# First layer of a two-layer trunk on one core: startup transfers, two projections' weights in the gated buffer, rotation's scaling on ACT, retention's scores two tiles ahead

## The chip, the core and the metric

The kernel runs on one core of a Trainium2 chip. The core has a matrix engine (PE, with its weight loads listed as PEld), a vector engine (DVE), an activation engine (ACT), a general engine (POOL) and a queue engine (SP). Each works through its own instructions in order and waits on semaphores for the others; transfers run on 16 DMA engines. The metric is the device time of one execution in microseconds (us); the median of several runs counts.

## The reference, cut to what matters

One inference step over 576 tokens (a prompt of 512 and 64 tokens of a running stream), width 1024, fp32. Layer 0 runs four heads of mLSTM and four heads of retention behind one input projection; layer 1 is latent attention; each is followed by a SwiGLU network.

```
z = x @ w_in_a     # mLSTM q, k, v, o; gates i, f; retention q, k, v, g
q, k = rope(q_ret, pos), rope(k_ret, pos)          # rotation
S_t = gamma_h * S_{t-1} + k_t^T v_t ; o_t = q_t S_t # retention, per head
h_ret = head_norm(o) * g_ret ; y = concat(h_mlstm, h_ret * silu(g)) @ w_out_a
```

Retention is computed in chunks: scores q k^T under a mask with the decay, times v, plus the state's part. The powers of gamma that belong to single rows are put into q and k right after the rotation: this is the "scaling" below.

## The kernel before, in words

Every fp32 product is made as three products of reduced-precision parts. A number is split into a high part (ACT casts it) and a low part (DVE subtracts, or POOL in other stages). For weights `split` does this (`L364` on ACT, `L362` on DVE), for x `split_x` (`L600`, `L601`, tiles `Xh`, `Xl`). Weights arrive in blocks of 512 KB through three raw buffers (`dma_w`, `L342`); a block is split in pieces ("fills") of 512 columns into slots of a ring (tiles `r0` to `r8`). Where a fill goes, and whether a slot is free, `claim` decides from the last fill that is still needed (`hold`); `pins` binds a fill to given slots, `L0_SLOTS` lists those of layer 0. `prefetch` emits splits ahead of use, up to `lead` fills.

The tokens stand in five tiles: tile 0 is the stream's 64, tiles 1 to 4 have 128 each. x comes in two halves, of 320 and 256 tokens; the first holds tiles 0 to 2, the second (x') tiles 3 and 4. What each engine does in which order follows from the order in which the program emits it. The stretch around the change runs so:

1. `rqrk`, retention's q and k: tiles 1 and 2 are multiplied k block by k block while weights and x arrive. Then the gates' product over the first half (`gate_mm(0)`), tile 0, tile 3, `gate_mm(1)`, tile 4. `tm_units` emits each tile as two units of four k blocks; `ev_qk` takes a finished tile out of its PSUM bank (`mm`): DVE rotates it (`L697` to `L700`) and scales q (`L702`) and k (`L704`), and a unit later PE transposes both (`L533`) and ACT copies the result to `qkT` (`L714`).
2. The gates: ACT copies their rows out of PSUM (`L660`) and PE transposes them; a task (`gates`, `L829` to `L911`) goes on with them, next to the following projections.
3. `rv` and `mv`, the values of retention and mLSTM, five tiles each. During `mv` five tasks of `retention` are interleaved, one for each tile: `s1` (scores in two PSUM banks, DVE multiplies by the mask, `L928`), `s2` (scores times values plus the state, the state's update, `L950` to `L959`, and the head norm, `L964` to `L970`) and `s3` (transposes and a copy).
4. Then mLSTM's `mk`, `mq`, `mo` and the gate `rg`, head by head.

PSUM has three banks called `mm`, four called `x` and one called `o`. The buffer `H` will hold the gated values; it is not in use this early, but for the columns from 8192 on. `T0`, `T1` and `Z` are working buffers with several uses one after another.

Of the kernel before, what the change touches and what calls it, by code (L numbers as in the profile page):

```python
# [8 lines left out]
F32 = mybir.dt.float32  # L9
# [8 lines left out]
KT = 8  # L18
# [19 lines left out]
NT = 5  # L38
# [7 lines left out]
RING = range(16)  # L46
LOW = range(8)
OUT_SLOTS = (range(8, 10), range(14, 16), range(10, 12), range(12, 14))
L0_SLOTS = (0, 1, 2, 3, 4, 5, 6, 7, 14, 15)
MLA_SLOTS = range(6)  # L50
LEAD = 5
LEAD_SLOTS = (8, 9, 14, 15, 0, 1, 2, 3, 4, 5, 6, 7)
# [165 lines left out]
class Kern:  # L218
    def __init__(self, ctx, tc, t):
        self.tc, self.nc, self.t = tc, tc.nc, t  # L220
        self.sb = ctx.enter_context(tc.tile_pool(name="sb", bufs=1))
        self.pm = ctx.enter_context(tc.tile_pool(name="pm", bufs=PM, space=bass.MemoryType.PSUM))
        self.px = ctx.enter_context(tc.tile_pool(name="px", bufs=PX, space=bass.MemoryType.PSUM))
        self.po = ctx.enter_context(tc.tile_pool(name="po", bufs=1, space=bass.MemoryType.PSUM))
        ctx.enter_context(tc.manual_schedule())
        self.n = 0
        self.bg = []
        self.clk = 0.0
        self.plan = Plan()
# [195 lines left out]
    def prefetch(self, i, lead, qlead=QLEAD):  # L425
        last = len(self.plan.fills) - 1
        self.load()
        while True:
            while self.split_next in self.done:
                self.split_next += 1  # L430
            j = self.split_next
            if j > min(i + (lead if j > last or len(self.plan.fills[j]) == 3 else qlead), last):
                return
            if not self.attempt(j):
                assert j > i, (i, self.hold, self.slot_of, self.plan.fills[j][0] in self.raws, self.pins.get(j))
                return
# [117 lines left out]
    def setup(self):  # L554
        nc, t = self.nc, self.t
        self.lead = LEAD
        self.lo_engine = nc.vector
        self.tk = TK0
        self.Z = self.st("Z", [128, KT * NTOK])
        self.T0 = self.st("T0", [128, T0_N])  # L560
        self.T1 = self.st("T1", [128, T1_N])
        self.Xh = self.st("Xh", [128, KT * NTOK], F32R)
        self.Xl = self.st("Xl", [128, KT * NTOK], F32R)
        self.H = self.st("H", [128, 2 * KT * NTOK], F32R)
        self.small = self.st("small", [128, 480])
# [12 lines left out]
        nc.gpsimd.memset(self.cvec[:, 2:4], 1.0 / 512.0)  # L578
        self.wgp = self.st("wgp", [128, KT, 16], F32R)
        for j in range(4):  # L580
            for k in (2 * j, 2 * j + 1) if j == 0 else (2 * j,):
                e = k + 1 if j == 0 else k + 2
                nc.sync.dma_start(half_view(self.Z, 0, k, e), half_dram(t["x"], 0, k, e))
                if j < RAW and k % 2 == 0:
                    self.dma_w(j, 2 if j == 0 else 1)

        x = self.obank()
        for _ in range(8):
            self.mm(x[:, 0:128], self.ones, self.ones, True, True)
# [4 lines left out]
        self.nc.scalar.copy(hi, wg)  # L594
        self.nc.vector.tensor_tensor(self.wgp[:, :, 8:16], wg, hi.bitcast(F32), ALU.subtract)

    def split_x(self, half, ks):
        for k in ks:
            a, b = hcols(half, k)
            self.nc.scalar.copy(self.Xh[:, a:b], self.Z[:, a:b])  # L600
            self.nc.vector.tensor_tensor(self.Xl[:, a:b], self.Z[:, a:b], self.Xh[:, a:b].bitcast(F32), ALU.subtract)  # L601

    def xs(self, half, cut=HN[0]):
        def f(k):
# [17 lines left out]
    def layer0(self):  # L622
# [38 lines left out]

        half_sum = Z[0:64, 3972:4484]

        def tm_units(name, evac, tiles=range(NT)):
            for i in tiles:
                box = {}

                def first(i=i, box=box):
                    self.rel = i == NT - 1
                    if i == 0 and name != "rqrk":  # L670
                        self.start((name, 0))
# [11 lines left out]
        def ev_qk(i, ps):  # L683
# [14 lines left out]
            V.tensor_tensor(t2[:, :, 0:32], p3[:, :, 32:64], S[:, :, 0:32].to_broadcast([L, 8, 32]), ALU.mult)  # L698
            V.tensor_tensor(t2[:, :, 32:64], p3[:, :, 0:32], S[:, :, 32:64].to_broadcast([L, 8, 32]), ALU.mult)  # L699
            V.tensor_tensor(t1, t1, t2, ALU.add)  # L700
            gam = self.cst[0:L, 0:8].unsqueeze(2)
            V.tensor_tensor(t1[:, 0:4, :], t1[:, 0:4, :], gam[:, 0:4, :].to_broadcast([L, 4, 64]), ALU.mult)  # L702
            kt = self.ktok[0:L, i, :].rearrange("p (h d) -> p h d", h=4)
            V.tensor_tensor(kt, t1[:, 4:8, :], gam[:, 4:8, :].to_broadcast([L, 4, 64]), ALU.mult)  # L704

            def g():
                x = self.xbank()
# [27 lines left out]

        self.XS = self.H[:, 8192:9216].rearrange("p (k t) -> p k t", k=KT)
        banks = [None, self.bank(), self.bank()]
        for k in range(KT):
            self.lead = 1 - k % 2 if k < KT - 1 else LEAD
            self.split_x(0, [k])  # L740
            if k == KT - 1:
                self.split_wg()
                self.split_x(1, range(KT))
            if k % 4 == 3:
                self.pair_sample(k - 3, k + 1)
            for i in (1, 2):
                self.tm(banks[i][0:TLEN[i], :], "rqrk", [k], self.xt(i), first=k == 0, last=k == KT - 1)
                if k == KT - 1:
                    ev_qk(i, banks[i])
            if k == 3:  # L750
                for name in ("rope", "ident", "mask", "cst"):
                    nc.sync.dma_start(getattr(self, name), t[name])
                nc.sync.dma_start(T0[:, 4300:4364], t["wg"])
                nc.sync.dma_start(self.bif, t["b_if"].to_broadcast([128, 8]))
            if k in (3, 4):
                j = k - 3
                nc.sync.dma_start(half_view(Z, 1, 4 * j, 4 * j + 4), half_dram(t["x"], 1, 4 * j, 4 * j + 4))
        for dst, name in ((self.sel, "sel"), (self.reset, "reset"), (self.m0, "m0"), (self.CxS, "c0"), (self.S[0], "s0"),
                          (self.gv, "gv"), (self.lnv, "lnv")):
            nc.sync.dma_start(dst, t[name])  # L760
        nc.gpsimd.tensor_scalar(self.gv, self.gv, 0.5, None, ALU.mult)
        gate_mm(0)
        tm_units("rqrk", ev_qk, (0,))
        tm_units("rqrk", ev_qk, (3,))
        gate_mm(1)
        self.gates_done = False
        self.spawn(self.gates(grow), 1.0)
        tm_units("rqrk", ev_qk, (4,))
        tm_units("rv", ev_rv)
        rt = self.retention()  # L770
        for g in rt:
            self.spawn(g)
# [3 lines left out]

        for x in (mva[64:128, 0], mvb[64:128, 0], r7[64:128, 1290:1418], r6[:, 1029:1157]):
            nc.gpsimd.memset(x, 0.0)
        tm_units("mv", ev_mv)

        done = set()
        self.ml_done = [0] * 4
# [131 lines left out]
    def retention(self):  # L914
# [5 lines left out]

        def s1(i):
            L, s = TLEN[i], TSTART[i]
            for o, bank in enumerate((self.obank(), self.bank())):
                x3 = bank[:, 0:256].rearrange("p (a t) -> p a t", a=2)
                p0 = 64 * o
                for a in range(2):
# [4 lines left out]
        def s2(i):  # L931
# [19 lines left out]
            for a in range(2):  # L951
                for p0 in (0, 64):
# [32 lines left out]
        self.ret_at = at  # L985

        def task(i):
            while at["s1"] < i or at["s2"] < i - 1 or self.qk_done < NT:
                yield
            s1(i)  # L990
            at["s1"] += 1
            yield LAG["r1"]
            while at["s2"] < i or at["s3"] < i - 1:
                yield
            if at["t2"] + LAG["r3"] > self.clk:
                yield at["t2"] + LAG["r3"] - self.clk
            s2(i)
            at["s2"] += 1
            at["t2"] = self.clk
            yield LAG["r2"]  # L1000
# [1262 lines left out]
```

## Time and profile before

| | us |
|---|---|
| median of 3 runs | 1393.08 (1391.89 to 1393.73) |
| the profiled execution | 1393.54 |
| its span, first to last instruction | 1391.6 |
| PE busy | 1351.7 |
| DVE busy | 979.5 |
| ACT busy | 610.8 |

Busy time is the time in which an engine has an instruction at work; the span is a little shorter than the execution, which has a start and an end around it. The mean clock granted to PE is 0.992 of full speed. In the lists below a row of the timeline gives start, length, engine, line of the program, operation, output and inputs, and in brackets the idle time of that engine just before it, with the instruction that ended it. A row of waits gives the sum, the number and the longest.

### The profile page before, as it was taken

Reading aid. Unit: us, or ns where it says so; the run is one execution under the profiler, and the core shown is the slowest. Engines: PE = TensorE matmul, PEld = TensorE weight load, DVE = VectorE, ACT = ScalarE, POOL = GpSimd, SP = SyncE. Lnnn points to the kernel's source line nnn. Section 1 sums busy time; section 2 is a strip of 40 time slices with the busy share of each in tenths; the row PEclk is TensorE's granted clock in tenths of the full one; section 3 lists DMA queues with packets and bytes.
Section 4 is the critical chain, followed back from the end, with each engine's and each line's share of the span. In section 5 each row is a group of like instructions: output and inputs, shape, how many; then the busy total and the mean of one; then the engine's idle time right before and its main releaser. Section 6 shows DMA issues by size and latency. Waiting matters only on the chain.

```text
span 1391.6 us, 24628 instructions
## 1 busy us (share of the span) xinstructions
PE 1351.7 (97%) x9759; PEld 1305.6 (94%) x9759; DVE 979.5 (70%) x2277; ACT 610.8 (44%) x1295; POOL 155.0 (11%) x182
## 2 busy tenths in 40 slices
PE   8999999999999999999999999999999999999995
PEld 6778999999999999999987899999999999999995
DVE  6757677678873685588898565667888358647876
ACT  4422333445551453255354466543555235425533
POOL 1100001115000000000021533311320000000000
PEclk9999999999999999999999999999999999999997
DMA  6121122611232123223321000021213312222221
GB/s 218 61 61 55 47 75 59 194 60 61 88 108 79 62 103 109 76 92 95 117 86 59 31 31 31 32 92 44 94 61 108 106 61 92 91 91 77 93 75 68
DMA packets 38234, 112.91 MB, mean 81 GB/s; under 512 B 5024, under 2 KB 12512, under 8 KB 38120
## 3 DMA queue, kind: packets, MB, share of 16 engines
q1 hardware_dynamic: 38120, 111.35, 24.3%
q8 instruction: 76, 1.25, 0.4%
q14 instruction: 38, 0.31, 0.1%
HBM read 107.45 MB, written 3.89 MB: 80 GB/s over the span
## 4 chain that ended last, share of the span: by engine, by line
PE 83%; DVE 10%; ACT 3%; DMA 2%; issue 2%; POOL 0%; SPq 0%; POOLq 0%; ACTq 0%; DVEq 0%
PE mm L465 44%; PE x L465 36%; PE x L533 2%; DVE r L362 2%; DVE Z L1279 1%; DMA raw<-in_w 1%; DVE Z L1265 1%; PE o L465 1%; ACT Xh L1311 1%; DMA Z<-in_x 1%; ACT r L364 0%; ACT Z L1318 0%; DVE small L542 0%; DVE small L541 0%; DVE small L543 0%
## 5 line engine op out<-in xcount | busy, mean ns | idle before, releaser
L465 PE MATMUL mm<-H,r 128*128 128x320 f32 (+2 forms) x2832 | 387.6, 297 | 0.0
L465 PEld LDWEIGHTS mm<-H,r 128*128 128x128 f32 x2832 | 378.3, 189 | 0.3
L465 PE MATMUL x<-Xh,r 128*128 128x288 f32 x1216 | 244.7, 296 | 0.0
L465 PE MATMUL mm<-Xh,r 128*128 128x288 f32 (+2 forms) x1152 | 229.2, 297 | 6.4 <-DVE Z L1185 2.8
L364 ACT CAST r<-raw 128x512 fp32r<-128x512 f32 (+2 forms) x292 | 178.0, 646 | 104.6 <-PE mm L465 76.0
L362 DVE TENSOR_TENSOR r<-raw,r 128x512 fp32r<-128x512 f32 (+2 forms) x276 | 194.4, 733 | 38.0 <-ACT r L364 37.8
L465 PE MATMUL x<-r,r 128*128 128x288 f32 (+2 forms) x1534 | 211.7, 293 | 0.2 <-DVE r L1055 0.2
L465 PEld LDWEIGHTS x<-r,r 128*128 128x128 f32 x1534 | 205.9, 188 | 0.5 <-DVE r L1055 0.5
L465 PEld LDWEIGHTS x<-Xh,r 128*128 128x128 f32 x1216 | 194.6, 188 | 0.5
L465 PEld LDWEIGHTS mm<-Xh,r 128*128 128x128 f32 x1152 | 183.4, 189 | 7.7 <-ACT Z L1318 3.8
L465 PE MATMUL x<-Xl,r 128*128 128x288 f32 x608 | 179.5, 295 | 0.0
L465 PE MATMUL mm<-Xl,r 128*128 128x288 f32 (+2 forms) x576 | 167.1, 298 | 0.0
L364 ACT CAST r<-T 128x512 fp32r<-128x512 f32 (+1 forms) x114 | 86.9, 762 | 127.5 <-DVE T L397 112.0
L465 PEld LDWEIGHTS x<-Xl,r 128*128 128x128 f32 x608 | 114.1, 188 | 0.0
L362 DVE TENSOR_TENSOR r<-T,r 128x512 fp32r<-128x512 f32 (+1 forms) x114 | 96.3, 866 | 18.6 <-ACT r L364 18.6
L465 PEld LDWEIGHTS mm<-Xl,r 128*128 128x128 f32 x576 | 107.2, 189 | 0.1
L465 PE MATMUL mm<-r,Xh 128*128 128x512 f32 (+1 forms) x320 | 98.8, 391 | 4.6 <-DVE r L699 2.6
L1319 POOL TENSOR_TENSOR Xl<-Z,Xh 128x288 fp32r<-128x288 f32 (+2 forms) x36 | 30.7, 853 | 467.0 <-ACT Z L1318 466.5
L465 PEld LDWEIGHTS mm<-r,Xh 128*128 128x128 f32 x320 | 58.8, 192 | 17.9 <-issue 3.0
L1223 ACT ACTIVATE T<-Z 128x288 f32<-128x288 f32 (+2 forms) x56 | 24.8, 443 | 91.8 <-DVE Z L1185 47.4
L465 PE MATMUL mm<-r,Xl 128*128 128x512 f32 (+1 forms) x160 | 61.3, 383 | 0.0
L1580 DVE TENSOR_TENSOR T<-T,x 128x288 f32<-128x288 f32 x38 | 17.2, 453 | 59.1 <-PE x L465 59.1
(316 smaller groups left out, 1725.9 us busy)
## 6 DMA issues: line engine op xcount, KB each, us to landing
raw<-in_w SPq DMA_DIRECT2D x169, 512.0 KB, 3.5
r<-in_w SPq DMA_DIRECT2D x20, 512.0 KB, 3.4
Z<-in_x SPq DMA_DIRECT2D x1, 1280.0 KB
o_y<-Z SPq DMA_DIRECT2D x2, 640.0 KB, 3.3
Z<-in_x SPq DMA_DIRECT2D x2, 512.0 KB, 7.2
Z<-in_x SPq DMA_DIRECT2D x1, 1024.0 KB, 8.7
o_y<-Z SPq DMA_DIRECT2D x4, 256.0 KB, 2.1
Z<-in_x SPq DMA_DIRECT2D x3, 320.0 KB, 4.9
```

The costliest lines, as they stand in the source:

```text
L362: self.lo_engine.tensor_tensor(t[:, 1], src, t[:, 0].bitcast(F32), ALU.subtract)
L364: self.nc.scalar.copy(t[:, 0], src)
L465: self.nc.tensor.matmul(out, lhsT, rhs, start=start, stop=stop, skip_group_check=more)
L533: self.nc.tensor.transpose(out, in_, self.ident[0:n, 0:n])
L1223: nc.scalar.activation(q, z, AF.Square)
L1265: V.tensor_tensor(z, z, xd[:, 0:n], ALU.subtract)
L1279: V.scalar_tensor_tensor(z, z, gain(m), R[:, 0:n], ALU.mult, ALU.mult)
L1311: A.activation(self.Xh[:, a:b], z, AF.Identity, bias=bias(m))
L1319: G.tensor_tensor(self.Xl[:, a:b], z, self.Xh[:, a:b].bitcast(F32), ALU.subtract)
L1580: V.tensor_tensor(s[:, 0:n], s[:, 0:n], ps, ALU.add)
```

## The change

*Transfers.* The first three transfers of x go out on ACT's queue, the weights on SP's alone. x' is loaded into `T1` right after the first k block is emitted, ahead of the tables (`rope`, `ident`, `mask`, `cst`), the gates' weights and biases. Before, it came behind these, into `Z`.

*Slots.* The fills of `rqrk` and `mv` are pinned to `H`, so that all ten slots of the ring serve `rv` and what comes after `mv`. A new bound, `cap`, limits how far ahead splits are emitted.

*Splits of x'.* Half of them follow the rotation of tile 1, half that of tile 2; before, all eight stood ahead of both.

*Scaling.* Instead of two DVE multiplications a tile, eight ACT instructions, each over 64 columns with a factor per row.

*Retention.* The scores of tile 1 use an `x` bank, so those of tile 0 and 1 need not share `o`. `s2` is cut in two, and the scores of tile i+2 are emitted between the state's update and the norm (`s2b`).

```diff
-L0_SLOTS = (0, 1, 2, 3, 4, 5, 6, 7, 14, 15)
+L0_SLOTS = (6, 7, 14, 15, 0, 1, 2, 3, 4, 5)
...
+        self.cap = len(self.plan.fills)
+        for k in range(KT):
+            for nm in ("rqrk", "mv"):
+                self.pins[self.where[(nm, k)][0]] = (len(RING) + k,)
...
-            if j > min(i + (lead if j > last or len(self.plan.fills[j]) == 3 else qlead), last):
+            if j > min(i + (lead if j > last or len(self.plan.fills[j]) == 3 else qlead), last, max(i, self.cap)):
...
-                nc.sync.dma_start(half_view(self.Z, 0, k, e), half_dram(t["x"], 0, k, e))
+                (nc.scalar if j < 2 else nc.sync).dma_start(half_view(self.Z, 0, k, e), half_dram(t["x"], 0, k, e))
...
+                    self.cap = self.where[(name, KT - 1)][0] + ahead * (1 if len(tiles) == 1 else i + 1)
...
-            gam = self.cst[0:L, 0:8].unsqueeze(2)
-            V.tensor_tensor(t1[:, 0:4, :], t1[:, 0:4, :], gam[:, 0:4, :].to_broadcast([L, 4, 64]), ALU.mult)
-            V.tensor_tensor(kt, t1[:, 4:8, :], gam[:, 4:8, :].to_broadcast([L, 4, 64]), ALU.mult)
+            for j in range(8):
+                nc.scalar.activation(t1[:, j, :] if j < 4 else kt[:, j - 4, :], t1[:, j, :], AF.Copy, scale=self.cst[0:L, j:j + 1])
...
-                self.split_x(1, range(KT))
+        for i in (1, 2):
+            ev_qk(i, banks[i])
+            self.split_x(1, range(4 * i - 4, 4 * i), x1)
...
-        tm_units("rqrk", ev_qk, (0,))
-        tm_units("rqrk", ev_qk, (3,))
+        self.lead = 2 * KT
+        tm_units("rqrk", ev_qk, (0,), 2)
+        tm_units("rqrk", ev_qk, (3,), 5)
...
-            for o, bank in enumerate((self.obank(), self.bank())):
+            for o, bank in enumerate((self.xbank() if i == 1 else self.obank(), self.bank())):
...
-            s2(i)
+            O = s2(i)
+            if i + 2 < NT:
+                s1(i + 2)
+            s2b(i, O)
```

PE's instructions keep their number and order; some read other tiles. Three places show what moves on the two engines that feed PE. Names are those of the tiles with numbers that tell their uses apart; `x4` stands for four alike. First ACT around the copy of the second gates (`T<-x 16x256`), before:

```order
L364 CAST r_35_231<-raw_30_145 128x512
L364 CAST r_36_234<-raw_30_145 128x512
L660 COPY T_3_71<-x_265 16x320
L527 COPY Z_69<-mm_283 64x512
L714 COPY Z_69<-x_321 128x4x128
L714 COPY Z_69<-x_327 128x4x128
L660 COPY T_3_71<-x_351 16x256
L714 COPY Z_69<-x_382 128x4x64
```

The same stretch of ACT now:

```order
L371 CAST r_33_284<-raw_28_151 128x512 x2
L534 COPY Z_69<-mm_283 64x512
L713 ACTIVATE r_24_112<-r_24_112,cst_83 64x64 x4
L713 ACTIVATE Z_69<-r_24_112,cst_83 64x64 x4
L371 CAST r_36_322<-raw_29_175 128x512
L371 CAST r_37_325<-raw_29_175 128x512
L371 CAST r_39_330<-raw_30_197 128x512
L723 COPY Z_69<-x_345 128x4x128
L723 COPY Z_69<-x_351 128x4x128
L713 ACTIVATE r_24_112<-r_24_112,cst_83 128x64 x4
L713 ACTIVATE Z_69<-r_24_112,cst_83 128x64 x4
L668 COPY T_3_71<-x_381 16x256
```

Between the two gate copies stood three copies; now the scaling of tile 0 and of tile 3 and five casts of weights stand there too. Second, DVE after the rotation of tile 1, before:

```order
L601 TENSOR_TENSOR Xl_73<-Z_69,Xh_72 128x256 x8
L362 TENSOR_TENSOR r_35_231<-raw_30_145,r_35_231 128x512
L362 TENSOR_TENSOR r_36_234<-raw_30_145,r_36_234 128x512
L697 TENSOR_TENSOR r_24_112<-mm_113,rope_82 128x512
L698 TENSOR_TENSOR r_24_112<-mm_113,rope_82 128x8x32
L699 TENSOR_TENSOR r_24_112<-mm_113,rope_82 128x8x32
L700 TENSOR_TENSOR r_24_112<-r_24_112 128x512
L702 TENSOR_TENSOR r_24_112<-r_24_112,cst_83 128x256
L704 TENSOR_TENSOR Z_69<-r_24_112,cst_83 128x256
L697 TENSOR_TENSOR r_24_112<-mm_114,rope_82 128x512
```

and now:

```order
L707 TENSOR_TENSOR r_24_112<-mm_113,rope_82 128x512
L708 TENSOR_TENSOR r_24_112<-mm_113,rope_82 128x8x32
L709 TENSOR_TENSOR r_24_112<-mm_113,rope_82 128x8x32
L710 TENSOR_TENSOR r_24_112<-r_24_112 128x512
L609 TENSOR_TENSOR Xl_73<-T_3_71,Xh_72 128x256 x4
L707 TENSOR_TENSOR r_24_112<-mm_114,rope_82 128x512
```

The rotation of tile 1 (`mm_113`) has moved ahead of the splits of x', of which four follow it, and its scaling has left this engine. Third, DVE in retention, the end of tile 2's norm, before:

```order
L970 TENSOR_SCALAR r_24_112<-x_872,small_75 128x128
L970 TENSOR_SCALAR r_24_112<-x_873,small_75 128x128
L928 TENSOR_TENSOR r_24_112<-o_909,mask_81 128x2x128
L928 TENSOR_TENSOR r_24_112<-mm_910,mask_81 128x2x128
L950 TENSOR_TENSOR Z_69<-Z_69,cst_83 128x256
```

and now:

```order
L986 TENSOR_SCALAR r_24_112<-x_914,small_75 128x128
L986 TENSOR_SCALAR r_24_112<-x_915,small_75 128x128
L369 TENSOR_TENSOR r_39_330<-raw_67_688,r_39_330 128x512 x2
L962 TENSOR_TENSOR Z_69<-Z_69,cst_83 128x256
L971 SCALAR_TENSOR_TENSOR Z_69<-x_984,cst_83,Z_69 64x128 x2
```

The masks of the scores to come have left this place (they stand ahead of the norm now), and two splits of weights have come to it, as they have after tiles 1 and 3; before, these splits followed the norm of tile 4.

More of the change, by code (lines that the diff above doesn't have):

```diff
@@ L326, in slot @@
     def slot(self, s):
+        if s >= len(RING):
+            o = 2 * FILL * (s - len(RING))
+            return self.H[:, o:o + 2 * FILL].rearrange("p (e c) -> p e c", e=2)
         b = self.buffer(s)
@@ L595, in split_wg, with split_x @@
         self.nc.vector.tensor_tensor(self.wgp[:, :, 8:16], wg, hi.bitcast(F32), ALU.subtract)
-    def split_x(self, half, ks):
+    def split_x(self, half, ks, src=None):
         for k in ks:
             a, b = hcols(half, k)
-            self.nc.scalar.copy(self.Xh[:, a:b], self.Z[:, a:b])
-            self.nc.vector.tensor_tensor(self.Xl[:, a:b], self.Z[:, a:b], self.Xh[:, a:b].bitcast(F32), ALU.subtract)
+            x = self.Z[:, a:b] if src is None else src[:, k, :]
+            self.nc.scalar.copy(self.Xh[:, a:b], x)
+            self.nc.vector.tensor_tensor(self.Xl[:, a:b], x, self.Xh[:, a:b].bitcast(F32), ALU.subtract)
     def xs(self, half, cut=HN[0]):
@@ L662, in layer0, with tm_units @@
         half_sum = Z[0:64, 3972:4484]
-        def tm_units(name, evac, tiles=range(NT)):
+        def tm_units(name, evac, tiles=range(NT), ahead=LEAD):
             for i in tiles:
@@ L737, in layer0 @@
         banks = [None, self.bank(), self.bank()]
+        x1 = T1[:, 0:KT * HN[1]].rearrange("p (k t) -> p k t", k=KT)
         for k in range(KT):
-            self.lead = 1 - k % 2 if k < KT - 1 else LEAD
+            self.lead = 1 - k % 2
             self.split_x(0, [k])
@@ L747, in layer0 @@
                 self.tm(banks[i][0:TLEN[i], :], "rqrk", [k], self.xt(i), first=k == 0, last=k == KT - 1)
-                if k == KT - 1:
-                    ev_qk(i, banks[i])
-            if k == 3:
+            if k == 0:
+                for j in range(2):
+                    nc.sync.dma_start(x1[:, 4 * j:4 * j + 4, :], half_dram(t["x"], 1, 4 * j, 4 * j + 4))
+            if k == 1:
                 for name in ("rope", "ident", "mask", "cst"):
@@ L754, in layer0 @@
                 nc.sync.dma_start(self.bif, t["b_if"].to_broadcast([128, 8]))
-            if k in (3, 4):
-                j = k - 3
-                nc.sync.dma_start(half_view(Z, 1, 4 * j, 4 * j + 4), half_dram(t["x"], 1, 4 * j, 4 * j + 4))
+        for i in (1, 2):
+            ev_qk(i, banks[i])
+            self.split_x(1, range(4 * i - 4, 4 * i), x1)
         for dst, name in ((self.sel, "sel"), (self.reset, "reset"), (self.m0, "m0"), (self.CxS, "c0"), (self.S[0], "s0"),
@@ L767, in layer0 @@
         self.spawn(self.gates(grow), 1.0)
-        tm_units("rqrk", ev_qk, (4,))
-        tm_units("rv", ev_rv)
+        tm_units("rqrk", ev_qk, (4,), 8)
+        tm_units("rv", ev_rv, ahead=2)
         rt = self.retention()
@@ L778, in layer0 @@
             nc.gpsimd.memset(x, 0.0)
-        tm_units("mv", ev_mv)
+        tm_units("mv", ev_mv, ahead=2)
+        self.cap, self.lead = len(self.plan.fills), LEAD
         done = set()
@@ L959, in s2, with s2b @@
                         V.scalar_tensor_tensor(to, up, dec, to, ALU.mult, ALU.add)
+            return O
+        def s2b(i, O):
+            L = TLEN[i]
             bs = self.smalls(24).rearrange("p (h c) -> p h c", h=4)
@@ L987, in task @@
         def task(i):
[L988 to L992, printed above, removed]
+            if i < 2:
+                while at["s1"] < i or self.qk_done < NT:
+                    yield
+                s1(i)
+                at["s1"] += 1
+                yield LAG["r1"]
             while at["s2"] < i or at["s3"] < i - 1:
```

## The prediction

> **What bounds the kernel now.** I read the page first, then PE's list of waits over the first 140 us (the diff touches nothing later), then the timelines of PE, DVE and ACT there, and last the windows with the granted clock.
>
> ```profile
> span 1391.6 us, 24628 instructions
> ...
> PE 1351.7 (97%) x9759; PEld 1305.6 (94%) x9759; DVE 979.5 (70%) x2277; ACT 610.8 (44%) x1295; POOL 155.0 (11%) x182
> ```
>
> PE is busy for 97% of the span, so an edit that issues the same matmuls in the same order can only win PE's waits back, or add to them. The waits that the change is near:
>
> ```profile
> PE o L465 <- DVE r L928: 2.7, 2, 1.4
> PE mm L465 <- DVE r L699: 2.6, 1, 2.6
> PE mm L465 <- DVE r L362: 1.4, 2, 1.2
> ```
>
> Together 6.7 us of 1391.6, half a per cent, and these rows are the whole stake apart from the clock. PE's timeline gives them their places (start, length, operation; the bracket is the idle time just before and what ended it):
>
> ```profile
> 18.97 0.31 PE L465 MATMUL x<-Xh,wgp 128*16 128x320 f32 x1
> ...
> 21.32 3.89 PE L465 MATMUL mm<-r,H 128*128 128x512 f32 x16
> 27.82 1.20 PE L465 MATMUL mm<-r,Xh 128*128 128x512 f32 x2 [2.61 <-DVE r L699]
> ...
> 32.11 0.27 PE L533 MATMUL x<-ident,r 128*128 128x128 f32 x1
> ...
> 32.90 0.71 PE L465 MATMUL mm<-r,Xh 128*128 128x512 f32 x2
> ...
> 40.92 0.45 PE L533 MATMUL x<-ident,T 16*64 16x16 f32 x5
> 41.31 0.73 PE L465 MATMUL mm<-r,Xh 128*128 128x512 f32 x2
> ...
> 44.21 2.31 PE L465 MATMUL mm<-r,H 128*128 128x512 f32 x8
> ...
> 50.01 1.71 PE L465 MATMUL mm<-r,H 128*128 128x512 f32 x5 [1.19 <-DVE r L362]
> 51.56 0.63 PE L465 MATMUL mm<-r,Xh 128*128 128x512 f32 x2
> ...
> 80.18 0.37 PE L465 MATMUL o<-Z 64*128 64x128 f32 x1 [1.40 <-DVE r L928]
> ...
> 94.72 0.37 PE L465 MATMUL o<-Z 64*128 64x128 f32 x1 [1.28 <-DVE r L928]
> ...
> 122.92 1.28 PE L533 MATMUL mm<-ident,r 128*128 128x128 f32 x4 [0.25 <-DVE r L970]
> 123.95 0.54 PE L465 MATMUL mm<-Xh,r 128*128 128x320 f32 x2
> ```
>
> In words: tile 0's projection runs from 21.32; tile 3 waits at 27.82 until DVE has rotated tile 1 out of the PSUM bank; tile 4's second half starts at 41.31, behind the second gate transpose (40.92); the values of retention (rv) start at 44.21 with tile 0 and wait for weight splits; at 80.18 the scores of tile 1 wait for their bank, at 94.72 those of tile 3; the first mLSTM projection starts at 123.95. The wait at 27.82 costs more than itself:
>
> ```profile
> 24.10:27.51 3.41, 1.11 (x5) 0.56 (x3) 3.40 (x8) 2.40 (x6) 0.00 (x0) 1.00 0.08 11
> 27.51:30.92 3.41, 3.10 (x7) 2.51 (x8) 3.31 (x8) 0.00 (x0) 0.00 (x0) 0.50 0.81 236
> ...
> 307.40:310.81 3.41, 1.70 (x13) 1.73 (x14) 3.37 (x8) 2.91 (x8) 2.96 (x4) 1.00 0.11 44
> ```
>
> Columns: the stretch, its length, then busy time of PE, PEld, DVE, ACT, POOL, then PE's granted clock. A stretch of 3.41 us with 1.11 us of PE work is followed by one of 3.41 us at clock 0.50. One with 1.70 us of work (307.40) kept 1.00 itself.
>
> **The change part by part.** Rows for the two engines that feed PE, DVE first:
>
> ```profile
> 25.11 1.30 DVE L362 TENSOR_TENSOR r<-raw,r 128x512 fp32r<-128x512 f32 x2
> 26.33 0.69 DVE L697 TENSOR_TENSOR r<-mm,rope 128x512 f32<-128x512 f32 x1
> ...
> 28.43 0.42 DVE L702 TENSOR_TENSOR r<-r,cst 128x256 f32<-128x256 f32 x1
> ...
> 29.11 0.68 DVE L697 TENSOR_TENSOR r<-mm,rope 128x512 f32<-128x512 f32 x1
> ```
>
> ```profile
> 16.92 0.25 ACT L594 CAST wgp<-T 128x64 fp32r<-128x64 f32 x1 [1.85 <-DMA T<-in_wg]
> 20.50 1.33 ACT L600 CAST Xh<-Z 128x256 fp32r<-128x256 f32 x4 [3.33 <-DMA Z<-in_x]
> ...
> 24.46 1.14 ACT L364 CAST r<-raw 128x512 fp32r<-128x512 f32 x2
> ...
> 37.84 0.36 ACT L660 COPY T<-x 16x256 f32<-16x256 f32 x1 [4.03 <-PE x L465]
> ```
>
> ```profile
> L1052 ACT ACTIVATE r<-x,T 128x128 f32<-128x128 f32 x16 | 5.7, 355 | 1.5 <-PE x L465 1.5
> L1298 ACT ACTIVATE Z<-Z,lnv 128x256 f32<-128x256 f32 x6 | 2.9, 531 | 2.1 <-POOL Z L1291 2.1
> L600 ACT CAST Xh<-Z 128x256 fp32r<-128x256 f32 x8 | 2.7, 404 | 4.7 <-DMA Z<-in_x 4.7
> ```
>
> *Scaling on ACT (5 tiles).* Out go two DVE multiplies a tile, 28.43 to 29.11: 0.68 us. In come eight ACT instructions of 128x64 with a scale per partition. No row shows one. The 128x64 cast without such an operand takes 0.25; the operand adds 0.13 in the group rows (531 against 404 ns); four casts back to back step by (1.33 - 0.40) / 3 = 0.31, that is 0.09 under their 0.40. So the step lies between 0.16 (0.25 - 0.09, operand free) and 0.29 (all added); the 355 ns of L1052 at twice the width, less 0.05 for the width, less 0.09, gives 0.21. I take 0.24: eight cost 1.35 to 2.4 us, 2.0 taken. DVE's rotation becomes 28.43 - 26.33 = 2.1 us a tile, ACT's part comes behind it: 4.1 against 2.8 before.
>
> The Trainium skill, "ScalarE: Activation LUTs", section "What ACT_TABLE_LOAD costs", gives 186 ns plus 0.833 ns a column and some 93 ns for each pointer operand, by which my estimate is 0.33 us for one of these. The cast of 0.25 agrees with the part that has no pointer (0.24 by the page).
>
> *Splits of x' between the rotations.* Half of the second half of x is split after tile 1's rotation, half after tile 2's; before, all eight came first. So tile 3's bank comes free with DVE's rotation of tile 1, from about 18.5 (tile 1's last products, just ahead of the gate matmuls at 18.97) to 20.6. ACT: scaling to 22.6, four casts to 23.9, DVE's last difference 24.4. PE comes to tile 3 when tile 0 is through: 21.32 + 16 x 0.233 = 25.05. The 2.61 us of wait goes, and with it the slow stretch: 27.82 to 32.11 took 4.3 us for twelve products that take 2.8 at 0.233 each. Next late is the transpose of tile 2, which needs rotation 24.4 to 26.5 and scaling to 28.5; tile 3's second half then starts at 29.05 instead of 32.90: **-3.85**.
>
> *What that chain delays.* ACT's queue is in order, and the second gate copy (37.84, needed by the transposes at 40.92) now stands behind the scaling of tile 3. Its chain: casts of x' to 29.8; gate copy, two casts and the copy of tile 0, 0.4 + 1.05 + 0.6, to 31.8; DVE's add 0.7 and rotation of tile 0 to 34.6; ACT's scaling to 36.6; three weight casts to 38.3, the last DVE split to 39.0, rotation of tile 3 to 41.1, scaling to 43.1, copy to 43.5. PE, without a wait, is there at 29.05 + (40.92 - 32.90) = 37.1. It waits 6.4 us, and tile 4's second half starts at 43.9: **+2.6** against 41.31. The four scalings on this chain make it 40.9 at their low end and 45.1 at their high end.
>
> *The clock.* By the row at 24.10, 1.1 us of work in 3.41 us brings 0.50 for the next 3.41. The boundaries run on from 30.92 to 37.75, 41.16, 44.57, 47.98. The stretch from 37.75 has no PE work, that from 41.16 has 1.1 us: half clock until 47.98, so of 43.5 to 47.98 half is lost, **+2.2**.
>
> The Trainium skill, "TensorE: Matmul & The Clock Gate", Part 1, has the clock halve after at least one idle window of about 3.4 us, free-running, and return after a busy one. The row at 24.10 differs: that window was not idle and the clock still fell. By the page alone only 43.5 to 44.57 runs at half rate, and the term is an estimated +0.5.
>
> *More free ring slots (projections' weights in the gated buffer).* From 44.21 to 51.56 PE needs 16 x 0.233 for the products and 1.45 for the transposes, 5.2 of 7.35 us. The rest waits for splits that had no slot; with rv's blocks claimed ahead this goes: **-2.15**. The gates run up to four us later, since their transposes come at 43.5 and tile 4's rotation and scaling stand ahead of their copies:
>
> ```profile
> 63.12 0.68 ACT L897 ACTIVATE T<-T 4x576 f32<-4x576 f32 x1
> ```
> ```profile
> 65.98 0.71 PE L533 MATMUL x<-ident,T 128*128 128x128 f32 x5
> ```
>
> PE comes 2.2 us after ACT is through, and is itself 2.6 us later by then, which covers it: 0, up to +1 if the chain is longer.
>
> *Scores on another bank.* The wait at 80.18: **-1.4**. PE is then at +2.6 + 2.2 - 2.15 - 1.4 = +1.25.
>
> *Scores two tiles ahead.* The 1.28 at 94.72 goes, since the masks are issued before the norm. But DVE sets the end of this stretch:
>
> ```profile
> 88.19 0.43 DVE L950 TENSOR_TENSOR T<-T,cst 128x256 f32<-128x256 f32 x1 [3.71 <-PE x L465]
> ...
> 104.29 0.42 DVE L950 TENSOR_TENSOR Z<-Z,cst 128x256 f32<-128x256 f32 x1 [2.17 <-PE x L465]
> ...
> 122.45 1.37 DVE L970 TENSOR_SCALAR r<-x,small 128x128 f32<-128x128 f32 x4
> 123.73 1.89 DVE L362 TENSOR_TENSOR r<-raw,r 128x512 fp32r<-128x512 f32 x3
> ```
>
> From 88.19 to 123.73 it idles 2.17 us and a further 0.2. Before, the splits for mLSTM's weights stand behind the last norm (123.73); now six stand between the norms, 6 x 0.62 = 3.7 us. The idle hides 2.4 of it, and the 1.28 won on PE is not passed on: the last transposes and mLSTM come **+1.3** later (all hidden: -1.3; no idle left: +3.7).
>
> *Startup.* The first x blocks go out on ACT's queue, the second half of x ahead of the tables.
>
> ```profile
> 10.00:20.00 10.00, 9.78 (x44) 7.42 (x45) 6.50 (x12) 4.79 (x11) 2.44 (x4) 1.00 0.92 290
> ```
>
> The DMA engines are 92% busy here, so it is the bytes in front that count, and for the first matmuls those stay the same: 0, within 0.4 either way. x' comes sooner, the tables later, both ahead of 18.5.
>
> Sum: +2.6 + 2.2 - 2.15 - 1.4 + 1.3 = +2.55 on the profiled execution's 1393.54 (0.46 above the median of 1393.08): 1396.1, and **1395.6** beside the median. With the scaling's bounds: low end, tile 4 at 41.3 (0.0) and one slow stretch (+1.7), sum -0.55; high end, +4.2 and +1.45, sum +3.4. Its own range is 1392.5 to 1396.5.
>
> **The rivals.** *Faster:* the short activations overlap more than any row shows. If eight took 1.05 us (0.12 each), the copy ends at 39.7, tile 4's second half starts at 40.1 (-1.2), the gap of 2.5 us falls into two stretches and the clock stays, as in the stretch at 307.40. Sum -1.2 - 2.15 - 1.4 + 1.3 = -3.45, and -6 where the norms' splits hide as well: 1387 to 1390. For it: the eight follow each other and wait for nothing in between. Against: the casts of x' overlap by only 0.09. It decides below 1.1 us for eight.
>
> *Slower:* a second slow stretch, before the last retention transposes. PE is through with rv and mv some 3 us before DVE's last norm; if one 3.41 us stretch holds under about 1.3 us of work there, mLSTM starts at half clock, +1.7: 1397.3, up to 1398.5 with late gates. For it: the row at 24.10. Against: the wait may fall across two stretches. It decides at 2.1 us of idle time in one of them.
>
> *The page's clock:* only an idle window halves it; the sum is +0.85, 1393.9. For it: 307.40; against: 24.10.
>
> *The change does not free tile 3:* if x' or the tables came after 20.6, the wait at 27.82 would be back in part, but this chain would be late in any case, so it changes little, +0.5.
>
> **How the numbers follow.** A measurement of this kernel can tell about 0.2%, 2.8 us, from no change. My forecast has 0.48 (0.27 within 2.8 us, 0.21 above, as the line at 1395.9 runs through its upper part), the page's clock 0.10 (no change), the faster rival 0.28, the slower one 0.14. That makes 0.28 faster, 0.37 the same, 0.35 slower. The range for 8 in 10 reaches into both rivals: 1387 to 1399.
>
> **What would show it.** Right: tile 3 starts without a wait near 25 at clock 1.00; PE idle near 37 to 43 until ACT's copy of the second gates; granted clock 0.50 behind it; no wait near 50 and 80; DVE without idle time from 90 to 125, and a wait of some 2 to 3 us before the last transposes of retention. Wrong: the copy lands before 40, or eight activations take under 1.1 us (then 1390 or less), or the clock stays at 1.00.

## The result, and the profile after

The changed kernel takes 1405.6 us (median of 4 runs, 1403.85 to 1406.98) against 1393.28: 1.0089 of the time before, 95% interval 1.0072 to 1.0107. Forecast were 1395.6 and a range that ended at 1399. The change is slower by 12.3 us, almost five times the 2.5 us of the forecast. The profiled execution of it, 1406.98 us, is the slowest of the four.

The page of the profiled execution:

```profile
span 1405.2 us, 24656 instructions
...
PE 1357.0 (97%) x9759; PEld 1312.7 (93%) x9759; DVE 974.4 (69%) x2267; ACT 619.6 (44%) x1335; POOL 153.8 (11%) x182
```

The span grew by 13.6 us. PE runs the same 9759 matmuls in the same order, but for 36 of them shortly before retention's last transposes (see the end of the point on the scores), so each can be set beside itself in the run before. Its waits (line, releaser, sum, number, longest) name the new places:

```profile
PE x L472 <- DVE small L913: 4.6, 1, 4.6
PE x L540 <- ACT T L668: 4.3, 1, 4.3
...
PE mm L540 <- DVE r L986: 2.8, 1, 2.8
PE x L540 <- ACT Z L723: 1.9, 1, 1.9
```

The waits on `L928`, `L699` and `L362` of before, 6.7 us together, have all gone; 13.6 us of waits stand in their place. That this sum equals the growth of the span is chance: PE waits some 7 us more there, and the clock adds most of the rest. PE's timeline shows where:

```profile
24.52 0.61 PE L472 MATMUL mm<-H,Xh 128*128 128x512 f32 x2
...
38.65 0.33 PE L540 MATMUL x<-ident,T 16*64 16x16 f32 x3 [1.88 <-ACT Z L723]
43.29 0.39 PE L540 MATMUL x<-ident,T 16*128 16x16 f32 x2 [4.31 <-ACT T L668]
43.61 1.22 PE L472 MATMUL mm<-H,Xh 128*128 128x512 f32 x2
...
67.60 0.71 PE L540 MATMUL x<-ident,T 128*128 128x128 f32 x5
72.91 1.86 PE L472 MATMUL x<-small,T 4*128 4x5 f32 x8 [4.60 <-DVE small L913]
...
88.41 0.27 PE L472 MATMUL x<-Z 64*128 64x128 f32 x1
...
131.89 1.43 PE L540 MATMUL mm<-ident,r 128*128 128x128 f32 x4 [2.75 <-DVE r L986]
```

Beside the same instructions of before, in us:

| instruction | before | after | later by |
|---|---|---|---|
| tile 3, first half | 27.82 | 24.52 | -3.3 |
| tile 4, second half | 41.31 | 43.61 | +2.3 |
| rv, tile 0 | 44.21 | 47.84 | +3.6 |
| rv, tile 1 | 51.56 | 53.18 | +1.6 |
| gates' sum matmuls | 66.62 | 72.91 | +6.3 |
| retention's scores, tile 1 | 80.18 | 88.41 | +8.2 |
| scores, tile 3 | 94.72 | 101.50 | +6.8 |
| last transposes of retention | 122.92 | 131.89 | +9.0 |
| span | 1391.6 | 1405.2 | +13.6 |

Between the sum matmuls and the scores of tile 1 PE waits for nothing and yet falls back from +6.3 to +9.7 at 80.41: the granted clock. The clock's stretches of 3.41 us in the run after, first around the gate copies, then around the sum matmuls (columns as in the windows of before: PE's busy time comes first after the length, the clock stands third from the end):

```profile
36.33:39.74 3.41, 0.77 (x7) 0.53 (x7) 2.75 (x6) 2.73 (x6) 0.00 (x0) 1.00 0.16 18
...
39.74:43.16 3.42, 0.00 (x0) 0.00 (x0) 1.10 (x3) 2.19 (x10) 0.00 (x0) 0.50 0.37 138
43.16:46.57 3.41, 3.28 (x9) 2.67 (x10) 2.46 (x8) 2.13 (x7) 0.00 (x0) 0.50 0.30 54
...
67.05:70.46 3.41, 1.25 (x9) 0.81 (x7) 1.97 (x4) 3.38 (x7) 0.00 (x0) 1.00 0.10 18
...
70.46:73.87 3.41, 0.96 (x5) 0.96 (x5) 2.33 (x8) 1.33 (x3) 0.00 (x0) 0.50 0.75 253
73.87:77.29 3.42, 3.42 (x11) 2.92 (x11) 0.18 (x1) 0.00 (x0) 0.00 (x0) 0.50 0.54 189
77.29:80.70 3.41, 3.41 (x9) 2.64 (x9) 0.00 (x0) 0.47 (x1) 0.00 (x0) 0.50 0.00 0
```

Two stretches at half clock at the gate copies, three at the sum matmuls; the first of each falls wholly or mostly into PE's wait. A further one follows the last transposes (131.90 to 135.31).

Why the sum matmuls wait is read from DVE and ACT. DVE:

```profile
67.65 1.29 DVE L369 TENSOR_TENSOR H<-raw,H 128x512 fp32r<-128x512 f32 x2 [1.63 <-ACT H L371]
...
71.31 1.29 DVE L369 TENSOR_TENSOR H<-raw,H 128x512 fp32r<-128x512 f32 x2 [0.23 <-ACT H L371]
72.63 0.14 DVE L912 COPY small<-T 4x1 f32<-4x1 f32 x1
72.70 0.15 DVE L913 COPY small<-T 4x4 f32<-4x4 f32 x1
```

and ACT, whose two exponentials (`L908`, `L909`) are the last that these copies and the transposes need:

```profile
65.58 0.68 ACT L908 ACTIVATE T<-T 4x576 f32<-4x576 f32 x1 [0.39 <-DVE T L906]
66.29 0.68 ACT L909 ACTIVATE T<-T 4x576 f32<-4x576 f32 x1
67.00 1.14 ACT L371 CAST H<-raw 128x512 fp32r<-128x512 f32 x2
```

The copies' data are there at 66.26. They come at 72.63, behind six splits of mv's weights, whose casts stand behind the exponentials on ACT. In the run before the same two copies followed the gates' chain at once, and DVE's next split came 9 us later:

```profile
63.13 0.14 DVE L900 COPY small<-T 4x1 f32<-4x1 f32 x1 [0.27 <-ACT T L896]
63.20 0.24 DVE L901 COPY small<-T 4x4 f32<-4x4 f32 x1
...
72.05 2.13 DVE L362 TENSOR_TENSOR r<-raw,r 128x512 fp32r<-128x512 f32 x3 [4.17 <-ACT r L364]
```

The prediction had the exponentials' time about right and did not look at DVE's queue behind them.

### The profile page after: what moved, and what is told of

The parts are those of the page before. It is cut to its first block, busy times and chain, and to the rows that moved or that the text cites. A ratio compares the mean times of both kernels' runs of the same rounds, so it can differ in the third digit from the quotient of the medians.

```text
span 1405.2 us, 24656 instructions
## 1 busy us (share of the span) xinstructions
PE 1357.0 (97%) x9759; PEld 1312.7 (93%) x9759; DVE 974.4 (69%) x2267; ACT 619.6 (44%) x1335; POOL 153.8 (11%) x182
## 3 DMA queue, kind: packets, MB, share of 16 engines
q8 instruction: 76, 1.25, 0.4%
## 4 chain that ended last, share of the span: by engine, by line
PE 82%; DVE 11%; ACT 4%; issue 1%; DMA 1%; POOL 0%; POOLq 0%; ACTq 0%; DVEq 0%
PE mm L472 44%; PE x L472 36%; PE x L540 2%; DVE r L369 2%; DVE Z L1299 1%; DVE Z L1285 1%; PE o L472 1%; ACT Xh L1331 1%; ACT r L371 1%; ACT Z L1338 0%; DVE small L550 0%; DVE small L549 0%; DVE small L548 0%; ACT r L713 0%; ACT Z L713 0%
## 5 line engine op out<-in xcount | busy, mean ns | idle before, releaser
L472 PE MATMUL mm<-Xh,r 128*128 128x288 f32 (+2 forms) x1152 | 233.7, 301 | 6.3 <-DVE Z L1205 2.8
L371 ACT CAST r<-raw 128x512 fp32r<-128x512 f32 (+2 forms) x276 | 168.8, 648 | 96.6 <-PE mm L472 73.3
L369 DVE TENSOR_TENSOR r<-raw,r 128x512 fp32r<-128x512 f32 (+2 forms) x260 | 183.8, 736 | 34.9 <-ACT r L371 34.6
L472 PEld LDWEIGHTS mm<-Xh,r 128*128 128x128 f32 x1152 | 187.4, 193 | 7.7 <-ACT Z L1338 3.8
L472 PE MATMUL mm<-r,Xh 128*128 128x512 f32 (+1 forms) x192 | 57.3, 382 | 1.0 <-ACT Z L1338 1.0
L1629 DVE SCALAR_TENSOR_TENSOR Z<-Z,mm 128x320 f32<-128x320 f32 (+1 forms) x32 | 14.3, 453 | 59.2 <-PE mm L472 59.2
L1631 DVE TENSOR_TENSOR Z<-Z,mm 128x320 f32<-128x320 f32 (+1 forms) x32 | 14.5, 453 | 49.7 <-PE mm L472 49.7
```

The costliest lines, as they stand in the source:

```text
L369: self.lo_engine.tensor_tensor(t[:, 1], src, t[:, 0].bitcast(F32), ALU.subtract)
L371: self.nc.scalar.copy(t[:, 0], src)
L472: self.nc.tensor.matmul(out, lhsT, rhs, start=start, stop=stop, skip_group_check=more)
L1629: V.scalar_tensor_tensor(z, z, ALPHA, ps[:, 0:HN[half]], ALU.mult, ALU.add)
L1631: V.tensor_tensor(z, z, ps[:, 0:HN[half]], ALU.add)
```

## The experiments

Ratios are to the kernel before, each from runs on the same chip. The median of the kernel before lay between 1393.05 and 1394.12 us in these groups, so a difference of two medians below is good to about 1 us.

| kernel | median us | ratio (95%) |
|---|---|---|
| changed | 1405.60 | 1.0089 (1.0072 to 1.0107) |
| e1, decay copies first | 1397.20 | 1.0029 (1.0018 to 1.0040) |
| e2, scaling on DVE | 1393.13 | 1.0002 (0.9992 to 1.0011) |
| e3, second gate copy first | 1402.70 | 1.0064 (1.0047 to 1.0081) |
| e4, no splits between norms | 1402.73 | 1.0067 (1.0052 to 1.0082) |
| e5, e1 and e2 | 1388.04 | 0.9960 (0.9946 to 0.9974) |
| e6, e5, e4 and an earlier mLSTM | 1382.83 | 0.9920 (0.9902 to 0.9939) |
| e7, e1 and e3 | 1396.33 | 1.0017 (1.0008 to 1.0026) |
| e8, before with retention's part | 1394.06 | 1.0001 (0.9991 to 1.0011) |
| e9, waits filled (too much) | 1429.10 | 1.0255 (1.0238 to 1.0272) |
| e10, e6 with scaling on ACT | 1393.02 | 0.9993 (0.9983 to 1.0002) |
| e11, waits filled | 1401.56 | 1.0056 (1.0040 to 1.0073) |

**e1: the decay copies ahead of the splits.**

```diff
+        dec = self.smalls(5)[0:4, :]
+        V.tensor_copy(dec[:, 0:1], stk[32:36, 63:64])
+        V.tensor_copy(dec[:, 1:5], stk[32:36, 191::128])
         yield LAG["g2"]
-        dec = self.smalls(5)[0:4, :]
-        V.tensor_copy(dec[:, 0:1], stk[32:36, 63:64])
-        V.tensor_copy(dec[:, 1:5], stk[32:36, 191::128])
```

> The two small DVE copies of the gates' decay (dec, lines 912 and 913 of the changed kernel) are emitted ahead of the pause in the gates' task, so that they stand ahead of the six splits of mv's weights in DVE's queue; nothing else changes. Theory Q (queue): PE's 4.6 us at its sum matmul and the slow clock behind it (3.4 us) come from these two copies standing behind six splits, so both go: about 1405.6 - 7.7 = 1398, 1397 to 1399.5, PE's wait there under 0.5 us. Rival L (the gates' chain itself is late, because scaling on ACT delays it): the copies wait for ACT's exponentials, not for the splits, the wait stays above 3 us, 1404 to 1406.

Measured 1397.2, 8.4 us less than the change. PE's waits of e1 in the first 145 us:

```profile
PE x L540 <- ACT T L668: 4.3, 1, 4.3
PE mm L540 <- DVE r L986: 2.8, 1, 2.8
PE x L540 <- ACT Z L723: 1.9, 1, 1.9
```

The row of the small copies is gone, the others stand. PE's sum matmuls come 3.9 us sooner and the matmul that stood at 80.78 comes 7.5 us sooner: wait and clock, as theory Q has it. So two copies of four rows, 0.15 us each, at the wrong place in a queue cost 8 of the 12.3 us.

**e2: scaling on DVE.** The two multiplications of before instead of eight activations.

> The changed kernel with the rotation's scaling back on DVE, as two multiplications a tile; all other parts as changed. Theory A (scaling on ACT puts four round trips of about 2 us into one chain): the second gate copy ends near 36 instead of 43.2, PE's 1.9 and 4.3 us there go together with the slow clock behind them (1.1 us), the gates' chain comes some 9 us sooner, and the wait for the decay copies falls from 4.6 to 2 or 3 us with some slow clock left: 1392 to 1398. Rival B (the splits in between set the chain, not the scaling): the copy still ends after 40, PE waits at least 3 us, 1402 or more.

Measured 1393.1, 12.5 us less than the change and not to be told from before. Its waits:

```profile
PE x L472 <- DVE small L914: 3.3, 1, 3.3
PE mm L540 <- DVE r L987: 2.8, 1, 2.8
```

No row on the gate copy is left, and the copy itself ends at 33.21 instead of 43.23: theory A. The sum matmuls wait for the same small copies (now `L914`), as expected, since the six splits still stand ahead of them.

**e3: the second gate copy ahead of tile 3's scaling.**

```diff
-        tm_units("rqrk", ev_qk, (3,), 5)
-        gate_mm(1)
+        tm_units("rqrk", lambda i, ps: (gate_mm(1), ev_qk(i, ps)), (3,), 5)
```

> The changed kernel with the second gate product and its copy emitted ahead of tile 3's rotation and scaling, so that the copy stands ahead of tile 3's scaling in ACT's queue; PE's order is unchanged. If the two waits on the gates are in series on PE alone: the copy ends near 39.5 instead of 43.2, PE gains 4 us and about 1 us of slow clock, 1400 to 1401. If PE is bound by the gates' chain through DVE, which starts behind the same splits as now, PE reaches the sum matmul 5 us sooner and waits 5 us longer there: 1404 to 1407, wait at the decay copies of 8 to 10 us.

Measured 1402.7, between the two. PE's rows:

```profile
37.75 0.32 PE L540 MATMUL x<-ident,T 16*64 16x16 f32 x3 [1.89 <-ACT Z L723]
38.48 0.39 PE L540 MATMUL x<-ident,T 16*128 16x16 f32 x2 [0.41 <-ACT T L668]
47.77 1.18 PE L540 MATMUL x<-ident,small 64*4 64x64 f32 x9 [1.10 <-DVE small L860]
71.20 1.84 PE L472 MATMUL x<-small,T 4*128 4x5 f32 x8 [4.98 <-issue]
```

The 4.31 us are down to 0.41 and tile 4 starts 4.8 us sooner. Of that 2.8 us are lost again by 47.77, to the half clock behind the 1.89 us and to a wait for the gates' first DVE stage, which had not moved. At the sum matmuls the wait is 4.98 instead of 4.60. So the waits are partly in series on PE and partly one behind the other in the gates' chain; neither expectation was right.

**e4: no splits between retention's norms.** In the bound for `mv`, `i + 1` became `min(i + 1, 2)`: four fills of mLSTM's weights ahead, no more.

> The changed kernel with the bound on splits during mv held at four fills of mLSTM's weights, so that the six splits leave the stretch between retention's norms and follow the last norm, as before the change. Theory D (DVE sets the end of this stretch, and the splits lengthen it): the last transposes of retention no longer wait 2.75 us, the slow clock behind them (1.1 us) goes, mLSTM starts 3 to 3.5 us sooner: 1401.5 to 1403. Rival (the splits fill DVE's idle time, and the norms wait for PE): same time within 1 us, 1404.6 to 1406.6.

Measured 1402.7, inside the first range, but the rows say that most of it is not theory D. DVE's, of the change first, then of e4:

```profile
96.32 0.43 DVE L962 TENSOR_TENSOR T<-T,cst 128x256 f32<-128x256 f32 x1 [2.45 <-PE x L472]
...
131.42 1.37 DVE L986 TENSOR_SCALAR r<-x,small 128x128 f32<-128x128 f32 x4
```

```profile
96.00 0.43 DVE L962 TENSOR_TENSOR T<-T,cst 128x256 f32<-128x256 f32 x1 [2.46 <-PE x L472]
...
110.65 0.43 DVE L962 TENSOR_TENSOR Z<-Z,cst 128x256 f32<-128x256 f32 x1 [1.26 <-PE x L472]
...
125.50 0.42 DVE L962 TENSOR_TENSOR Z<-Z,cst 128x256 f32<-128x256 f32 x1 [1.59 <-PE x L472]
...
130.38 1.36 DVE L986 TENSOR_SCALAR r<-x,small 128x128 f32<-128x128 f32 x4
```

From the first state's update to the last norm's end rows: 35.1 us with the splits, 34.4 without, 34.3 before. Six splits of 0.62 us cost 0.7 to 0.8, since without them DVE waits 2.9 us for PE. PE still waits 2.1 us before the last transposes. The half clock behind them is gone in this run (mLSTM 1.9 us sooner in all); the rest of the difference lies after 300 us, where the slow stretches fall differently (below).

**e5: e1 and e2 together.**

> The changed kernel with both edits: rotation's scaling back on DVE, and the decay copies ahead of the splits. With scaling on DVE alone PE still waited 3.3 us for the decay copies and ran 6.8 us at half clock there. If that too is the order in DVE's queue: 3.3 plus up to 3.4 us go from 1393.1, 1386.5 to 1390, and PE's wait there is under 0.5 us. If with less scaling on ACT the copies wait for the exponentials instead: 1392 to 1394.

Measured 1388.0, 5.1 us less than e2, 0.996 of before. PE's wait for the copies is gone; behind the first 10 us one long wait is left:

```profile
PE mm L540 <- DVE r L987: 2.7, 1, 2.7
```

**e6: e5, the bound of e4, and mLSTM's first projection ahead of the last transposes.**

```diff
-                self.wait(lambda: self.ret_at["s3"] == NT)
+                self.wait(lambda: self.ret_at["s2"] == NT)
```

> Those two edits, no splits between retention's norms, and mLSTM's first projection allowed to start when the last scores are used, ahead of the last transposes of retention (they then come some 7 us later on PE). Theory T (PE's wait before the last transposes is the latency of the last norm on DVE, about 6 us from the state's update to the last row, with no PE work left behind it): with mLSTM's matmuls in that place the wait of 2 to 2.8 us and the slow clock go: 2 to 4 us under the kernel with the first two edits, 1383 to 1387. Rival (the wait only moves on, to mLSTM's own splits or copies, which stand behind the norm on DVE): within 1 us of that kernel.

Measured 1382.8, 5.2 us under e5 and 0.8% under before (0.9902 to 0.9939): theory T, a little beyond its 2 to 4 us; the bound of e4 has a part in it that no run separates. PE's waits in the first 145 us are now these two, at the very start:

```profile
PE mm L472 <- ACT H L371: 1.0, 1, 1.0
PE o L472 <- POOL ones L583: 1.0, 1, 1.0
```

The last transposes stand at 121.26, among mLSTM's matmuls, and wait for nothing. This version beats both kernels.

**e7: e1 and e3 together, scaling on ACT.**

> Scaling stays on ACT; the second gate copy stands ahead of tile 3's scaling and the decay copies ahead of the splits. Alone the first gave 2.9 us, since PE then waited 5 us for the decay copies. If the two waits of the gates hide each other, both edits together give more than their sum (2.9 + 8.4 = 11.3 us): about 1393, 1391.5 to 1394.5, and what scaling on ACT costs is mostly the place of these three small instructions. If the gates' chain itself is late: the wait stays above 2 us, 1396 or more.

Measured 1396.3, 0.9 us less than e1 alone (the intervals of the two ratios overlap), and outside the first range. The wait for the copies is gone, but not the rest:

```profile
PE x L540 <- ACT Z L723: 1.9, 1, 1.9
PE x L540 <- DVE small L860: 1.1, 1, 1.1
```

The half clock of 6.8 us (38.26 to 45.08) stayed too, with only this 1.9 and a further 0.4 us of wait close together. So mending the place of three small instructions does not make scaling on ACT free: beside e5 it costs 8.3 us.

**e8: the kernel before with retention's part alone.**

> The kernel before with the change to retention alone (scores of tile 1 on another bank, scores two tiles ahead). Its waits were 1.40 and 1.28 us. Theory T (the second only moves behind the last norm, since PE then reaches the last transposes sooner and the norms take as long): 1.4 us won, 1391.0 to 1392.2, and a wait of over 1 us before the last transposes. Rival (both won): 1390 to 1390.8.

Measured 1394.1, the same as before within 0.1%; the ranges of both theories are missed, and the mechanism of theory T is there:

```profile
PE mm L533 <- DVE r L974: 2.1, 1, 2.1
```

At 32 us PE leads the run before by 2.1 us, though the programs are the same up to there: tile 3's wait took 1.58 us instead of 2.61, and the clock stayed at 1.00 behind it (the stretch from 23.24 to 26.65 has 1.83 us of PE work, that at 24.10 of the run before 1.11). Against this, PE leads by 3.4 at tile 1's scores and 4.7 at tile 3's: 1.3 and 1.3 us won, both waits gone. At the last transposes the lead is 2.9. Scores two tiles ahead win 1.3 us and give back 1.8 behind the last norm. The remaining 0.8 us could not be seen in the time.

**e9 and e11: PE's waits at the gates filled with matmuls on ones.**

```diff
+        ob = self.obank()
+
+        def fill(n):
+            for _ in range(n):
+                nc.tensor.matmul(ob[:, 0:128], self.ones, self.ones, start=True, stop=True, skip_group_check=False)
+        fill(30)
         for i in range(NT):
+            if i == 3:
+                fill(72)
...
+        fill(72)
         for h in range(4):
             self.mm(x3[:, h * 8:h * 8 + 5], self.sel[:, h * 128:(h + 1) * 128], dec, True, True)
```

> The changed kernel with 174 more matmuls of 128x128 (ones by ones, 0.056 us each at full clock, results unused) in the places where PE waits: 30 ahead of the gates' transposes, 72 ahead of the fourth of them, 72 ahead of the sum matmuls. They take 1.7, 4.0 and 4.0 us, a little less than the waits (1.9, 4.3, 4.6). If PE's idle time is what halves the granted clock, the slow stretches from 39.7 to 46.6 and from 70.5 to 80.7 us go and with them 1.1 and 3.4 us: 1400 to 1402.5. If something else halves it, or matmuls on ones don't count as work: 1404 to 1407.

Measured 1429.1: a call on these plain fp32 tiles is two matmuls of 0.116 us, four times what the expectation put it at, so the fill was far longer than the waits. e11 has 7, 17 and 17 calls.

> The same with the number of added matmuls set by their measured price: one call on ones is two matmuls of 0.116 us, 0.23 us a call, so 7, 17 and 17 calls take 1.6, 3.9 and 3.9 us, inside the waits of 1.9, 4.3 and 4.6. If PE's idle time is what halves the granted clock: the slow stretches at 39.7 and 70.5 us go, with 1.1 and 3.4 us, 1400 to 1402.5. If it is not: 1404 to 1407.

Measured 1401.6, inside the first range. PE's rows:

```profile
38.26 4.06 PE L840 MATMUL o<-ones 128*128 128x128 f32 x34
...
67.05 3.96 PE L840 MATMUL o<-ones 128*128 128x128 f32 x34
72.27 1.05 PE L472 MATMUL x<-small,T 4*128 4x5 f32 x8 [1.26 <-DVE small L921]
```

The copies come as late as in the change. The two slow stretches at the gate copies are gone, of the three at the sum matmuls one is left (73.76 to 77.17, behind the 1.26 us). So it is PE's idle time that brought these stretches, and work of no use that fills it is worth some 2 us here: at the last of them (77.70, where the change has 79.99) e11 leads by 2.3 us, 0.5 of it from startup. The two spans differ by 5.7 us; the rest of it arises behind 130 us, where this run has fewer slow stretches, although its wait before the last transposes is 2.7 us too. The ratios' intervals of e11 and of the change just meet, so the size is rough.

**e10: e6 with scaling on ACT.**

> The fastest kernel so far (1382.8 us) with one edit undone: the rotation's scaling is on ACT again, as in the change. This prices the scaling where no other wait of the first layer is left. By the changed kernel's rows PE waits 1.9 and 4.3 us for ACT's copies again and runs 6.8 us at half clock at the gates (1.1 to 3.4 us): 7 to 10 us slower, 1390 to 1393. If the scaling costs only through the decay copies, which stand ahead of the splits here: 1383 to 1385.

Measured 1393.0: 10.2 us more than e6, the upper end of the first range. The wait for the second gate copy is back, as long as in the change:

```profile
PE x L540 <- ACT T L668: 4.3, 1, 4.3
```

PE is 6.7 us behind e6 at the fourth gate transpose and 8.2 where the half clock behind it ends (46.94), and the spans differ by 9.0. This part of the change alone undoes all that the others win.

## Why the prediction was wrong, point by point

*Tile 3's wait and its slow stretch* (predicted -3.85 at the second half): the wait went, and the second half came at 28.65 instead of 32.90, -4.25. Right.

*Scaling on ACT* (eight taken at 2.0 us): right. Four take 1.06 us, and the copy behind the eight of tile 3 starts 1.9 us after the first of them. The second gate copy, forecast to end at 43.5, ended at 43.23:

```profile
40.97 1.06 ACT L713 ACTIVATE r<-r,cst 128x64 f32<-128x64 f32 x4 [1.88 <-DVE r L710]
...
42.89 0.34 ACT L668 COPY T<-x 16x256 f32<-16x256 f32 x1
```

PE's second half of tile 4 came at +2.3 (predicted +2.6). The wait has two parts, since the first transposes waited 1.88 us for a PSUM bank that ACT had not yet emptied, which was not foreseen.

*The clock behind the gate copies* (+2.2): two slow stretches, as forecast, but they ended at 46.57 and not 47.98, and PE lost 1.3 us (from +2.3 to +3.6 at rv's tile 0). The boundaries are not those carried on from the run before. By the rows a stretch with 0.77 us of work was followed by half clock, too. The Trainium skill, "TensorE: Matmul & The Clock Gate", Part 1, calls the window free-running, and here the runs agree: the boundaries lie 1.4 us apart in the two runs. The idle window that the Trainium skill asks for there is too strict, since the stretch with 0.77 us was not idle. The 0.5 worked out from that rule came out too low for another reason, the boundaries: the stretch from 39.74 to 43.16 has no PE work, and with it the rule, too, gives half clock until 46.57.

*Ring slots* (-2.15): +3.6 at rv's tile 0 and +1.6 at its tile 1, so -2.0. Right.

***The gates*** (0, up to +1): **this is the step that failed.** The working read one row, ACT's last exponential, and asked whether PE would come after it. ACT was through at 66.97 and PE at 67.60, so that much held. But the matmul behind those transposes needs two DVE copies as well, and between the gates' two stages six splits of mv, which have their own slots in `H` now, came in ahead of them. From +1.6 to +6.3 it cost 4.7 us of waiting, and to +9.7 a further 3.4 of half clock: 8.1 together where 0 was put down. e1 took 8.4 us back by moving two instructions of 0.15 us. The working followed the data of the gates' chain, and not the queue that its small instructions stand in.

*Scores on another bank* (-1.4): from +9.7 to +8.2 here, 1.3 in e8. Right.

*Scores two tiles ahead, splits between the norms* (+1.3): from +8.2 to +9.0 at the last transposes, +0.8. The sign and the wait (2.75 us, forecast 2 to 3) were right, the reason only in part: e4 shows that the splits make up 0.7 to 0.8 us of it, and that 2.1 us of the wait stay without them. PE has too little work left beside the last norm, so what is won at tile 3's scores comes back there (e8); giving PE other work is what helps (e6).

PE's order, which was said to be kept, differs just here. The first row of mv's products behind tile 4's last state products, before and after:

```profile
116.36 0.73 PE L465 MATMUL mm<-r,Xh 128*128 128x512 f32 x2
```

```profile
125.68 0.73 PE L472 MATMUL mm<-H,Xh 128*128 128x512 f32 x2
```

Before, 24 products of mv run from there to the transposes at 122.06; in the change 12 run, to 128.54, and the other 12 stand ahead of tile 4's part of retention. The last transposes of tile 4 come 6.56 us behind these rows before and 6.21 after, so the norm takes no longer, but PE has 2.8 us less work to cover it, about the size of the wait. e4 and e8 have the new order and the wait as well. No run has the new scores in the old order, so this share is argued and not shown.

*Startup* (0 within 0.4): tile 0's matmuls start at 20.85 instead of 21.32, -0.5. Near enough.

Two further terms lay outside the sum. The slower rival, a slow stretch behind the last transposes, came in addition: 1.1 us. And after 300 us the clock was half in three stretches that before did not have (319.63, and 995.47 to 1002.30) and not in one that it had (798.92): net two of 3.41 us, each of which loses half of itself: 3.4 us. Nothing in that part of the program was changed, and the stretches fall differently in every kernel here: e1 has those at 801.94 and 989.67, e2 at 308.22 and 984.06, e6 only the one at 788.76. Among the four runs of e3, one program, the mean clock lay between 0.985 and 0.989 and the time between 1403.86 and 1400.32. So these 3.4 us look like luck, of where the boundaries fall on short waits, though all four runs of the change lay at 0.984 and 0.985; no run tests it. The sum then stands: forecast +2.55, the gates +8.1, the stretch behind the last transposes +1.1, the late stretches +3.4, the other terms -1.55 (the clock at the gate copies alone -0.9), together +13.6.

## What to carry to other kernels

Before an edit frees slots or lets work be issued sooner, list for each instruction that the busiest engine needs what then stands ahead of it in its own queue; a copy of 0.15 us behind six prefetched splits cost 8 us, and moving it brought them back. An operation moved to an engine with time to spare still makes a round trip, and a chain of such trips (four of 2 us here) can cost far more than the work saved, 10 us here for 3.4 us less of DVE work (0.68 a tile). Where PE waits for a last result, give it other work: e6 did that.

## What the runs showed of the hardware

The granted clock fell, or stayed low, after stretches of 3.41 us with 0.77, 0.96 and 1.25 us of PE work, not only after idle ones; in the run before one with 1.70 kept it and in e8 one with 1.83, but one with 2.27 (at 795.49 of the run before, small matmuls) did not, so busy time alone does not say it. The same stretch of program lost the clock in the run before (1.11 us of work) and kept it in e8 (1.83). One stretch that was busy throughout, 73.87 to 77.29, did not bring full clock back: its first 0.8 us were the sum matmuls on 4 rows and 5 columns. It returned after the next. The Trainium skill, "TensorE: Matmul & The Clock Gate", Part 1, has the clock back after one busy window; the stretch from 43.16 agrees, this one does not. A wait of 4.6 us thus cost 3.4 us more, and a wait of 1.26 us in e11 was still followed by one slow stretch.
